# Output weights scaled in the input projection and kept in DRAM, and one add per attention unit on GpSimd

## The chip, the cores and the metric

The kernel runs on one core of a Trainium2 chip. The metric is the device time of one execution in microseconds (us); three runs were made. The trace is that of one profiled execution. Engines are named as in the profile: PE is TensorE (its weight loads are PEld), DVE is VectorE, ACT is ScalarE, POOL is GpSimd, SP is SyncE, which here issues every DMA.

## The reference, cut to what matters

One encoder layer on 2048 tokens of width 1024. All of it is float32.

```python
mod = (silu(c) @ w_ada + b_ada)                 # one row of 6*1024
shift1, scale1, gate1, shift2, scale2, gate2 = split(mod, 6)
u = adaln_modulate(x, shift1, scale1)
q, k, v, glu = split(u @ w_in, ...)             # input projection
q, k = rope(rms_norm(q)), rope(rms_norm(k))
attn = rms_norm(softmax(q @ k.T / 8) @ v)       # 8 query heads, 2 kv heads of 64
h = conv_module(glu)                            # width 31, layer norm, swish, 512x512 projection
mixed = concat([attn, h]) @ w_o                 # 1024 x 1024
x = layer_norm(ALPHA * x + gate1 * mixed)
...                                             # gated MLP with a conv of width 3, second layer norm
```

Because `gate1` is one row, `gate1 * (m @ w_o)` is `m @ (w_o * gate1)`: the kernel multiplies the columns of `w_o` with `gate1` and never multiplies `mixed`.

## The kernel before, in words

A product that needs float32 accuracy is made of three matmuls on a high and a low part of each operand. `split` (L123, L126) makes the parts: ACT copies the tile to the high part, DVE (or POOL) subtracts it for the low part.

The work runs in stages. The program is written in Python generators, and the order on every engine is set at build time by a scheduler, which places an instruction once its operands are ready in its own time model. Each engine then runs its list strictly in order, and so does SP's list of DMAs.

- **Input projection** (to about 400 us). The 16 blocks of 128 tokens go through in groups; each group makes keys, queries and the two GLU halves, and prepares the block after it. Beside it the generator `ada_later` (L277) computes the modulation rows that are needed later, `gate1` first: for each row half of 512 columns eight loads of `w_ada` into `ar` (3 buffers), eight multiply-adds on DVE into `acc`, two matmuls with ones (L293, L294), which leave the row on all 128 partitions, and a store of one partition to `mod_d` (L297). After each group it is advanced by 7 steps.
- **Attention** (about 400 to 1250 us). 16 units, numbered 0 to 15 here, each for two heads (`p`) and 512 queries (`c`). `unit_main` goes over 16 key blocks `kt`: two score products (L576, L577), an exponential on ACT into `pr` (L578, 6 buffers), and, three key blocks at a time, the products with `v` (L587). The row sums are kept in two accumulators: POOL adds 12 of the 16 `pr` into `lp` and DVE the other 4 into `ld` (L605, L608); each has one buffer. After each key block `step` advances three generators: `unit_end` of the unit before, `unit_prep` of the unit after (its score maxima: L177 on PE, L179 on DVE, then L182, L186, L188), and `conv_work`.
- `unit_end` begins with `lp + ld` on DVE (L527); two steps later PE sums it over the partitions (L535), which frees `lp` for the next unit.
- `conv_work` ends, in unit 12, with `load_wo` (L618). It loads `gate1` on all partitions, then 16 pieces of `w_o` (tile `rw`, 2 buffers). Each piece is multiplied with `gate1` on DVE (L630) and split: ACT writes `woh` (L123), DVE writes `wol` (L126).
- **Output projection, MLP, last norm** (from about 1250 us) use the split weights and are not touched.

Of the kernel before, what the change touches and what calls it, by code (L numbers as in the profile page):

```python
# [10 lines left out]
F32 = mybir.dt.float32  # L11
F32R = mybir.dt.float32r
AF = mybir.ActivationFunctionType
ALU = mybir.AluOpType
# [4 lines left out]
P = 128  # L19
D = 1024  # L20
S = 2048
NT = 16
KD = D // P
# [10 lines left out]
def layer_kernel(ctx, tc, x, cT, w_ada, b_ada, b_adaT, w_in, qg2, kg2, rope, conv_t, cmask, mmask,  # L34
# [3 lines left out]
    V, A, G, T, SY = nc.vector, nc.scalar, nc.gpsimd, nc.tensor, nc.sync  # L38
# [15 lines left out]
    mod_d = dram.tile([4, D], F32, name="mod_d")  # L54
# [2 lines left out]
    t_d = dram.tile([2, 4, P, 4, 512], F32, name="t_d")  # L57
    g_d = dram.tile([NJ, P, S], F32, name="g_d")
    w_d = dram.tile([7, P, NJ // 2, 512], F32, name="w_d")

    ident = const.tile([P, P], F32, name="ident")
    make_identity(nc, ident)
# [131 lines left out]
    with ExitStack() as ph:  # L194
# [81 lines left out]
        def ada_later():  # L276

            for i, v in enumerate((2, 3, 4, 5)):
                for h in range(2):
                    c0 = v * D + h * 512  # L280
                    acc = wka.tile([P, 512], F32, name="acc", bufs=1)
                    for k in range(KD):
                        raw = wka.tile([P, 512], F32, name="ar", bufs=3)
                        SY.dma_start(raw, w_ada[k * P:(k + 1) * P, c0:c0 + 512])
                        if k == 0:
                            V.tensor_scalar(acc, raw, cs[:, 0:1], None, op0=ALU.mult)
                        else:
                            V.scalar_tensor_tensor(acc, raw, cs[:, k:k + 1], acc, op0=ALU.mult, op1=ALU.add)
                        yield
                    br = wka.tile([P, 512], F32, name="ar", bufs=3)  # L290
                    SY.dma_start(br[0:1, :], b_ada[0:1, c0:c0 + 512])
                    ps = bank()
                    T.matmul(ps, lhsT=ones, rhs=acc, start=True, stop=False)  # L293
                    T.matmul(ps, lhsT=ones[0:1, :], rhs=br[0:1], start=False, stop=True)  # L294
                    A.activation(acc[0:1], ps[0:1], AF.Identity, bias=1.0 if v == 4 else 0.0,
                                 scale=1 / ALPHA if v == 5 else 1.0)
                    SY.dma_start(mod_d[i:i + 1, h * 512:(h + 1) * 512], acc[0:1, :])  # L297
                    yield
# [153 lines left out]
        for gi, grp in enumerate(groups):  # L452
            ks = {}
            nxt = grp[-1] + 1
            last = gi == len(groups) - 1
            for s in grp:
                ks[s] = keys(s, us[s], proj(us[s], "kv", pss[s, "kv"], hi) if gi == 0 else None)
            for s in grp:
                queries(s, us[s], ks[s][0], proj(us[s], "q", pss[s, "q"], hi) if gi == 0 else None)
                if len(grp) == 1 and nxt < NT:  # L460
                    us[nxt] = prep(nxt)
            if last:
                for s in grp:
                    keys_end(s, ks[s][1])
                for _ in bg:
                    pass
                wix.close()
                u0 = pool(rx, "u0", "right")
                gen0 = unit_prep(u0, *units[0], prep0, u0)
                next(gen0)  # L470
                gen1 = unit_prep(None, *units[1], prep1, u0)
                next(gen1)
            for i, s in enumerate(grp):
                for _ in glu(s, us[s]):
                    if last:
                        drain(gen0, 4)
                if i == 0 and len(grp) > 1 and nxt < NT:
                    us[nxt] = prep(nxt)
                if not last:
                    keys_end(s, ks[s][1])  # L480
                if gi > 0:
                    for _ in range(7):
                        next(bg, None)
            if gi == len(groups) - 2:
                us[14] = prep(14)
                us[15] = prep(15)
# [37 lines left out]
    def unit_end(p, c, po, lp, ld):  # L524
        o = wk.tile([P, 512], F32, name="o", bufs=2)
        A.activation(o, po, AF.Copy)
        V.tensor_tensor(lp, lp, ld, op=ALU.add)  # L527
        osq = wk.tile([P, 512], F32, name="osq", bufs=1)
        A.activation(osq, o, AF.Square)
        ls = wk.tile([P, 8], F32, name="ls", bufs=2)  # L530
        yield
        yield
        pl = bank()
        for i in range(2):
            T.matmul(pl[i * 64:(i + 1) * 64, :], lhsT=ones[:, 0:64], rhs=lp[:, i, :], start=True, stop=True)  # L535
        l2 = wk.tile([P, 512], F32, name="l2", bufs=1)
        A.activation(l2, pl, AF.Square, scale=EPS ** 0.5)
        V.tensor_tensor(osq, osq, l2, op=ALU.add)
        yield
        yield  # L540
        st = bank()
        for i in range(4):
            T.matmul(st[:, i * 2:i * 2 + 2], lhsT=osq[:, i * P:(i + 1) * P], rhs=blk, start=True, stop=True)
        A.activation(ls, st[:, 0:8], AF.Copy)
        G.tensor_tensor(ls, ls, mhalf[:, 0:8], op=ALU.pow)
        for _ in range(5):
            yield
        rescale(wk, o, agc[:, p:p + 1], ls)
        SY.dma_start(mix_d[p, :, c * 512:(c + 1) * 512], o)
        yield  # L550
# [67 lines left out]
    def load_wo():  # L618
        wr = pool(wrx, "wr", "right")
        wp = pool(wox, "wpC", "right")  # L620
        g1 = wp.tile([P, D], F32, name="row_g1")
        SY.dma_start(g1, mod_d[0:1].broadcast_to([P, D]))
        for k in range(KD):
            woh.append(wp.tile([P, D], F32R, name="woh%d" % k))
            wol.append(wp.tile([P, D], F32R, name="wol%d" % k))
            for h in range(2):
                sl = slice(h * 512, (h + 1) * 512)
                raw = wp.tile([P, 512], F32, name="rw", bufs=2)
                SY.dma_start(raw, w_o[k * P:(k + 1) * P, sl])
                V.tensor_tensor(raw, raw, g1[:, sl], op=ALU.mult)  # L630
                yield
                split(woh[k][:, sl], wol[k][:, sl], raw)
                yield

        def load_mix(t):
            raw = wp.tile([P, KD, P], F32, name="mr", bufs=1)
            SY.dma_start(raw, mix_d[:, :, t * P:(t + 1) * P].rearrange("k p t -> p k t"))
            mh = wp.tile([P, KD, P], F32R, name="mh", bufs=2)
            ml = wp.tile([P, KD, P], F32R, name="ml", bufs=2)
            split(mh, ml, raw, None, G)  # L640
            mixes[t] = mh, ml

        mixes["load"] = load_mix
        mixes["raw"] = [wr.tile([P, KD, P], F32, name="wr%d" % i) for i in range(2)]
        load_mix(0)
        yield
        load_mix(1)
# [771 lines left out]
```

## Time and profile before

| what | value |
|---|---|
| time of the three runs | 2818.41, 2823.8, 2823.6 us; median 2823.6 |
| profiled execution: its own time | 2820.62 us |
| profiled execution: span of the trace | 2818.8 us |
| PE busy | 2680.5 us, 95% of the span |
| DVE busy | 2213.6 us, 79% |
| POOL busy | 1246.4 us, 44% |
| mean granted clock of PE | 0.977 of full speed |

PE is the busiest engine over the whole span. A busy share over the span says little about one stage; the stages that the change touches are read one by one further down. A granted clock of 1.00 is 2.4 GHz, one of 0.50 is 1.2 GHz.

### The profile page before, as it was taken

How to read it: one execution, taken by the hardware profiler on the slowest of the kernel's cores; microseconds unless marked ns; L12 is line 12 of the kernel's file. 1: busy time of each engine (PE TensorE's matmuls, PEld its weight loads, DVE VectorE, ACT ScalarE, POOL GpSimd, SP SyncE). 2: the span in 40 equal slices, each digit the busy share in tenths (PEclk: the TensorE clock that was granted, in tenths of full speed). 3: DMA queues.
4: the chain of work that ended last, by engine and by line, in shares of the span. 5: the costliest groups of instructions: out<-in, count | busy, mean ns of one | idle time of the engine just before them, and what ended most of it. 6: DMA issues, size and time to landing. Idle time of an engine off the chain costs nothing. (4 is left out here: it accounts for less than half of the span.)

```text
span 2818.8 us, 35305 instructions
## 1 busy us (share of the span) xinstructions
PE 2680.5 (95%) x12108; PEld 2020.6 (72%) x12108; DVE 2213.6 (79%) x3188; ACT 1304.3 (46%) x2562; POOL 1246.4 (44%) x914
## 2 busy tenths in 40 slices
PE   7999999999999999899988999999999998999996
PEld 6877866766565665458867788876888887777774
DVE  7554466576858767847779999899999878989999
ACT  4433324445545455434464554555554555443542
POOL 3534436886857667534544322233231002336235
PEclk8999999999999999899999999999999999999998
DMA  8343241010101112116777433354344226545542
GB/s 274 95 138 115 76 98 33 22 34 19 31 19 27 27 38 75 42 30 187 229 214 226 150 131 116 124 175 160 130 155 139 89 91 220 158 128 147 170 148 68
DMA packets 336867, 320.59 MB, mean 114 GB/s; under 512 B 70688, under 2 KB 244128, under 8 KB 336688
## 3 DMA queue, kind: packets, MB, share of 16 engines
q1 hardware_dynamic: 336688, 318.34, 37.3%
q8 instruction: 95, 1.56, 0.2%
q14 instruction: 84, 0.69, 0.1%
HBM read 225.71 MB, written 92.55 MB: 113 GB/s over the span
## 5 line engine op out<-in xcount | busy, mean ns | idle before, releaser
L1082 PE MATMUL b<-o,wh 128*128 128x512 f32 x3696 | 1155.3, 397 | 47.2 <-ACT wh L123 18.5
L1082 PEld LDWEIGHTS b<-o,wh 128*128 128x128 f32 x3696 | 698.8, 190 | 218.3 <-ACT wh L123 23.8
L1082 PE MATMUL b<-o,wl 128*128 128x512 f32 x1848 | 719.1, 396 | 6.5 <-DVE wl L126 6.5
L123 ACT ACTIVATE wh<-wr 128x512 fp32r<-128x512 f32 (+2 forms) x456 | 252.0, 571 | 379.2 <-PE b L1082 202.4
L608 POOL TENSOR_TENSOR lp<-lp,pr 128x1024 f32<-128x1024 f32 x152 | 382.4, 2516 | 77.5 <-ACT pr L578 69.5
L1082 PEld LDWEIGHTS b<-o,wl 128*128 128x128 f32 x1848 | 350.5, 190 | 90.9 <-DVE wl L126 12.7
L578 ACT ACTIVATE pr<-b 128x512 f32<-128x512 f32 x512 | 279.1, 599 | 290.6 <-PE b L577 283.3
L179 DVE TENSOR_REDUCE mm<-b 128x1 f32<-128x512 f32 x512 | 321.4, 681 | 116.2 <-PE b L177 114.6
L126 DVE TENSOR_TENSOR wl<-wr,wh 128x512 fp32r<-128x512 f32 (+2 forms) x456 | 334.7, 746 | 10.7 <-ACT wh L123 9.9
L587 PE MATMUL b<-pr,vt 128*64 128x512 f32 x1024 | 245.1, 609 | 4.2 <-ACT pr L578 4.2
L1178 POOL TENSOR_TENSOR cb<-cb,g 128x512 f32<-128x512 f32 x44 | 75.2, 1732 | 383.6 <-DMA cb<-in_w_down_dram 383.6
L576 PE MATMUL b<-q,K 128*128 128x512 f32 x512 | 219.1, 430 | 9.5 <-DVE mm L179 5.3
L577 PE MATMUL b<-q,K 72*128 72x512 f32 x512 | 207.2, 406 | 3.0 <-DVE q L188 3.0
L177 PE MATMUL b<-K,q 128*128 128x512 f32 x512 | 166.0, 421 | 6.0 <-DVE mm L179 5.0
L587 PEld LDWEIGHTS b<-pr,vt 128*64 128x64 f32 x1024 | 66.5, 138 | 131.2 <-issue 114.1
L126 POOL TENSOR_TENSOR o<-stg,o 128x512 fp32r<-128x512 f32 x53 | 82.5, 1558 | 148.2 <-ACT o L123 146.2
L177 PEld LDWEIGHTS b<-K,q 128*128 128x128 f32 x512 | 92.4, 192 | 71.4 <-issue 34.1
L123 ACT ACTIVATE o<-stg 128x512 fp32r<-128x512 f32 x177 | 107.6, 630 | 74.8 <-DMA stg<-w_d 52.8
L1059 POOL TENSOR_TENSOR wr<-wr,wr 128x384 f32<-128x384 f32 (+1 forms) x32 | 34.8, 1089 | 241.4 <-DVE s L1056 229.9
L576 PEld LDWEIGHTS b<-q,K 128*128 128x128 f32 x512 | 99.8, 195 | 57.5 <-issue 18.7
L577 PEld LDWEIGHTS b<-q,K 72*128 72x128 f32 x512 | 100.4, 196 | 21.0 <-issue 3.4
L126 DVE TENSOR_TENSOR o<-stg,o 128x512 fp32r<-128x512 f32 x124 | 109.3, 900 | 2.7 <-ACT o L123 2.5
(259 smaller groups left out, 4891.4 us busy)
## 6 DMA issues: line engine op xcount, KB each, us to landing
wr<-in_w_up_dram SPq DMA_DIRECT2D x88, 512.0 KB
stg<-w_d SPq DMA_DIRECT2D x133, 256.0 KB
g_d<-y SPq DMA_DIRECT2D x44, 512.0 KB
w_d<-cb SPq DMA_DIRECT2D x77, 256.0 KB
wr<-g_d SPq DMA_DIRECT2D x96, 192.0 KB
ar<-in_w_ada_dram SPq DMA_DIRECT2D x64, 256.0 KB
cb<-in_w_down_dram SPq DMA_DIRECT2D x44, 256.0 KB
x<-in_x_dram SPq DMA_DIRECT2D x32, 256.0 KB
```

Source lines behind the costliest of these rows:

```text
L123: A.activation(hi, src, AF.Copy)
L126: (el or V).tensor_tensor(lo, src, hi.bitcast(F32), op=ALU.subtract)
L177: T.matmul(px, lhsT=q1[:, i * P:(i + 1) * P], rhs=K1[:, g, kc * 512:(kc + 1) * 512], start=True, stop=True)
L179: V.tensor_reduce(mm[:, h * 4 + i, kc:kc + 1], px, axis=AX, op=ALU.max)
L576: T.matmul(ps, lhsT=k1, rhs=m1, start=True, stop=False)
L577: state["s"] = T.matmul(ps, lhsT=k2, rhs=m2[0:72], start=False, stop=True).ins
L578: ex = state["exp"] = A.activation(pr[:, i, :], ps, AF.Exp, scale=0.125).ins
L587: state["pv"] = T.matmul(po[i * 64:(i + 1) * 64, :], lhsT=vt[:, kt, g * 64:(g + 1) * 64], rhs=pr[:, i, :], start=kt == 0, stop=kt == NT - ...
L608: eng.tensor_tensor(acc, acc, pr, op=ALU.add)
L1059: (V if n < NU else G).tensor_tensor(a21, a11, a21, op=ALU.subtract)
L1082: T.matmul(ps, lhsT=a[x][:, k, :], rhs=b[y][k], start=first and k == 0 and (x, y) == (0, 0), stop=k == nk - 1 and x == 1, skip_group_check ...
L1178: G.tensor_tensor(b[i, k], b[i, k], g2[:, k * 512:(k + 1) * 512], op=ALU.mult)
```

## The change

In `ada_later` the two halves of the `gate1` row are no longer stored to `mod_d`. They are copied from PSUM on all 128 partitions, and then eight pieces of `w_o` per half are loaded into `ar`, multiplied on DVE and stored to a new DRAM tensor `wo_d`, one piece per step. `load_wo` loads the finished pieces into `rw`, with 4 buffers instead of 2, and only splits them; the broadcast load of `gate1` there is gone. `ada_later` is advanced by 9 steps per group instead of 7 (it had 72 steps and has 86). In `unit_end` the add `lp + ld` moves from DVE to POOL.

```diff
+    wo_d = dram.tile([2, KD, P, 512], F32, name="wo_d")
...
                     T.matmul(ps, lhsT=ones, rhs=acc, start=True, stop=False)
                     T.matmul(ps, lhsT=ones[0:1, :], rhs=br[0:1], start=False, stop=True)
+                    if v == 2:
+                        A.activation(acc, ps, AF.Copy)
+                        for k in range(KD):
+                            raw = wka.tile([P, 512], F32, name="ar", bufs=3)
+                            SY.dma_start(raw, w_o[k * P:(k + 1) * P, h * 512:(h + 1) * 512])
+                            V.tensor_tensor(raw, raw, acc, op=ALU.mult)
+                            SY.dma_start(wo_d[h, k], raw)
+                            yield
+                        continue
                     A.activation(acc[0:1], ps[0:1], AF.Identity, bias=1.0 if v == 4 else 0.0,
                                  scale=1 / ALPHA if v == 5 else 1.0)
...
                 if gi > 0:
-                    for _ in range(7):
+                    for _ in range(9):
                         next(bg, None)
...
         A.activation(o, po, AF.Copy)
-        V.tensor_tensor(lp, lp, ld, op=ALU.add)
+        G.tensor_tensor(lp, lp, ld, op=ALU.add)
         osq = wk.tile([P, 512], F32, name="osq", bufs=1)
...
         wp = pool(wox, "wpC", "right")
-        g1 = wp.tile([P, D], F32, name="row_g1")
-        SY.dma_start(g1, mod_d[0:1].broadcast_to([P, D]))
         for k in range(KD):
...
                 sl = slice(h * 512, (h + 1) * 512)
-                raw = wp.tile([P, 512], F32, name="rw", bufs=2)
-                SY.dma_start(raw, w_o[k * P:(k + 1) * P, sl])
-                V.tensor_tensor(raw, raw, g1[:, sl], op=ALU.mult)
+                raw = wp.tile([P, 512], F32, name="rw", bufs=4)
+                SY.dma_start(raw, wo_d[h, k])
                 yield
                 split(woh[k][:, sl], wol[k][:, sl], raw)
```

Three places show how the lists of the engines change. A row is the source line, the operation, output and inputs, the tile, and how often it repeats; numbers behind a tile's name count buffers. Line numbers from `ada_later` on are 10 higher after the change, and 7 higher from `load_wo` on.

The first place is DVE's list where unit 12 ends and unit 13 begins. Before:

```order
L608 TENSOR_TENSOR ld<-ld,pr 128x1024
L527 TENSOR_TENSOR lp<-lp,ld 128x1024
L630 TENSOR_TENSOR rw<-rw,row_g_9677 128x512
L169 TENSOR_TENSOR q_9743<-b,q_9742 64x512
L630 TENSOR_TENSOR rw<-rw,row_g_9677 128x512
L169 TENSOR_TENSOR q_9752<-b,q_9751 64x512
L179 TENSOR_REDUCE mm<-b 128x1 x2
L126 TENSOR_TENSOR wol_9680<-rw,woh_9679 128x512
L179 TENSOR_REDUCE mm<-b 128x1 x4
L126 TENSOR_TENSOR wol_9680<-rw,woh_9679 128x512
L630 TENSOR_TENSOR rw<-rw,row_g_9677 128x512
L179 TENSOR_REDUCE mm<-b 128x1 x6
```

And the same place after the change:

```order
L618 TENSOR_TENSOR ld<-ld,pr 128x1024
L127 TENSOR_TENSOR wol_9741<-rw,woh_9740 128x512 x2
L170 TENSOR_TENSOR q_9802<-b,q_9801 64x512
L180 TENSOR_REDUCE mm<-b 128x1
L127 TENSOR_TENSOR wol_9832<-rw,woh_9831 128x512
L180 TENSOR_REDUCE mm<-b 128x1
L170 TENSOR_TENSOR q_9811<-b,q_9810 64x512
L127 TENSOR_TENSOR wol_9832<-rw,woh_9831 128x512
L180 TENSOR_REDUCE mm<-b 128x1 x4
L127 TENSOR_TENSOR wol_9913<-rw,woh_9912 128x512 x2
L127 TENSOR_TENSOR wol_10018<-rw,woh_10017 128x512
L180 TENSOR_REDUCE mm<-b 128x1 x2
```

The add and the multiplies are gone, and the subtractions follow each other more closely: before, the 16 of them were spread over unit 13 and the beginning of unit 14; now the last stands ahead of the last 12 of the 32 reductions `mm` of unit 13. On ACT the last of the 16 copies `woh` now has 18 of the unit's 32 exponentials behind it.

The second place is POOL's list at the end of unit 0 (`tz` are the conv's weights, `hT` its input with zeroed edges). Before:

```order
L608 TENSOR_TENSOR lp<-lp,pr 128x1024 x7
L668 MEMSET hT 128x4
L669 MEMSET hT 128x4
L676 TENSOR_TENSOR tz<-ct,cm 128x384 x4
L668 MEMSET hT 128x4
```

And after:

```order
L618 TENSOR_TENSOR lp<-lp,pr 128x1024 x7
L537 TENSOR_TENSOR lp<-lp,ld 128x1024
L675 MEMSET hT 128x4
L676 MEMSET hT 128x4
L683 TENSOR_TENSOR tz<-ct,cm 128x384 x4
```

The add of the two sums now stands in POOL's list directly behind the last sum of the unit, ahead of the conv's work.

The third place is DVE's list in one group of the input projection. Before:

```order
L384 TENSOR_TENSOR K_93<-b,K_93 64x2x128
L347 TENSOR_REDUCE kss<-ka 128x2
L348 TENSOR_SCALAR kss<-kss 128x2
L352 TENSOR_TENSOR kn<-b,krst 128x128
L375 TENSOR_TENSOR kd<-kb,kr 128x256
L347 TENSOR_REDUCE qss<-qa 128x8
L348 TENSOR_SCALAR qss<-qss 128x8
L126 TENSOR_TENSOR ul<-u,uh 128x512
```

And after:

```order
L394 TENSOR_TENSOR K_94<-b,K_94 64x2x128
L301 TENSOR_TENSOR ar<-ar,acc 128x512 x3
L357 TENSOR_REDUCE kss<-ka 128x2
L358 TENSOR_SCALAR kss<-kss 128x2
L362 TENSOR_TENSOR kn<-b,krst 128x128
L301 TENSOR_TENSOR ar<-ar,acc 128x512
L385 TENSOR_TENSOR kd<-kb,kr 128x256
L301 TENSOR_TENSOR ar<-ar,acc 128x512 x2
L357 TENSOR_REDUCE qss<-qa 128x8
L358 TENSOR_SCALAR qss<-qss 128x8
L301 TENSOR_TENSOR ar<-ar,acc 128x512
L127 TENSOR_TENSOR ul<-u,uh 128x512
```

The multiplies of `w_o` stand between the keys' work (`kss`, `kn`, `kd`) and the low parts `ul` of the next block's input; what follows a multiply on DVE waits with it.

## Rows read from the trace of the kernel before

**Rows 1.** The page's busy times: engine, us, share of the span, instructions.

```profile
PE 2680.5 (95%) x12108; PEld 2020.6 (72%) x12108; DVE 2213.6 (79%) x3188; ACT 1304.3 (46%) x2562; POOL 1246.4 (44%) x914
```

**Rows 2.** Stretches: length, PE, PEld, DVE, ACT, POOL busy us (instructions), clock, DMA.

```profile
100.00:350.00 250.00, 248.89 (x1249) 201.96 (x1248) 119.89 (x236) 89.55 (x198) 105.10 (x137) 1.00 0.33 104
741.20:786.50 45.30, 42.99 (x187) 24.80 (x186) 35.26 (x47) 23.43 (x43) 34.66 (x16) 0.96 0.09 24
1099.40:1165.90 66.50, 51.77 (x188) 28.18 (x189) 63.69 (x71) 30.61 (x56) 35.85 (x14) 0.86 0.25 78
1165.90:1211.50 45.60, 45.37 (x187) 24.26 (x184) 35.75 (x50) 22.71 (x43) 30.65 (x12) 0.94 0.05 18
```

**Rows 3.** Waits from 1090 to 1260 us: waiter, whom for, us, times, longest.

```profile
PE b L576 <- DVE mm L179: 3.4, 2, 2.8
PE b L587 <- ACT pr L578: 3.4, 2, 2.4
```

**Rows 4.** Tile `rw`: min/median/max ns of the subtractions; idle time before its instructions.

```profile
L126 DVE TENSOR_TENSOR wol<-rw,woh x16: 672/692/2280, 1104.3 to 1177.6; 128x512 fp32r<-128x512 f32 x16
...
  DVE rw L630: 18.0, 9
```

**Rows 5.** DVE's costliest groups in unit 13: busy us, mean ns, idle before.

```profile
L630 DVE TENSOR_TENSOR rw<-rw,row_g 128x512 f32<-128x512 f32 x14 | 20.3, 1448 | 0.6 <-DMA rw<-in_w_o_dram 0.6
L179 DVE TENSOR_REDUCE mm<-b 128x1 f32<-128x512 f32 x32 | 19.9, 674 | 0.0
L126 DVE TENSOR_TENSOR wol<-rw,woh 128x512 fp32r<-128x512 f32 x13 | 14.9, 1147 | 2.2 <-ACT woh L123 2.1
```

**Rows 6.** Stretches at the lower clock, columns as in group 2.

```profile
1164.30:1171.10 6.80, 5.77 (x14) 1.57 (x14) 6.62 (x11) 5.20 (x11) 0.00 (x0) 0.50 0.18 56
450.90:457.70 6.80, 4.24 (x16) 3.98 (x17) 3.70 (x5) 0.39 (x1) 0.44 (x1) 0.50 0.00 0
```

**Rows 7.** Timeline of DVE, end of unit 0: start, us, [idle before].

```profile
451.37 1.22 DVE L527 TENSOR_TENSOR lp<-lp,ld 128x1024 f32<-128x1024 f32 x1 [7.15 <-POOL lp L608]
452.63 1.28 DVE L169 TENSOR_TENSOR q<-b,q 64x512 fp32r<-64x512 f32 x2
```

**Rows 8.** Timeline of PE at the same place.

```profile
453.46 0.77 PE L695 MATMUL b<-tz,hT 128*128 128x128 f32 x2 [4.75 <-DVE q L169]
```

**Rows 9.** Line L527: min/median/max ns; what it waited for (us, times).

```profile
L527 DVE TENSOR_TENSOR lp<-lp,ld x16: 1205/1226/2114, 451.4 to 1243.4; 128x1024 f32<-128x1024 f32 x16
...
  POOL lp L608: 16.5, 6
```

**Rows 10.** Waits of PE from 440 to 900 us: us, times, longest.

```profile
PE b L186 <- DVE mz L182: 4.7, 2, 2.6
...
PE b L177 <- DVE mm L179: 2.2, 1, 2.2
PE b L576 <- DVE mm L179: 1.9, 2, 1.7
```

**Rows 11.** Tile `lp`: POOL's adds, min/median/max ns.

```profile
L608 POOL TENSOR_TENSOR lp<-lp,pr x152: 2338/2385/3281, 411.4 to 1238.4; 128x1024 f32<-128x1024 f32 x152
```

**Rows 12.** Timeline of DVE, end of unit 14.

```profile
1211.44 1.23 DVE L527 TENSOR_TENSOR lp<-lp,ld 128x1024 f32<-128x1024 f32 x1 [2.26 <-POOL lp L608]
```

**Rows 13.** Timeline of PE at the same place.

```profile
1213.28 1.08 PE L535 MATMUL b<-lp,ones 128*64 128x512 f32 x4
```

**Rows 14.** Waits of DVE from 100 to 350 us: us, times, longest.

```profile
DVE acc L286 <- DMA mod_d<-acc: 15.1, 6, 3.3
DVE acc L288 <- DMA ar<-in_w_ada_dram: 10.8, 19, 1.1
```

**Rows 15.** Timeline of POOL in unit 13.

```profile
1103.41 2.59 POOL L126 TENSOR_TENSOR ml<-mr,mh 128x1024 fp32r<-128x1024 f32 x1 [4.04 <-ACT mh L123]
```

**Rows 16.** Timeline of DVE at the same place.

```profile
1104.27 2.28 DVE L126 TENSOR_TENSOR wol<-rw,woh 128x512 fp32r<-128x512 f32 x1
```

## The prediction

> **What bounds the kernel now.** I began with the page's busy times: PE works 95% of the span [rows 1], so the time can only fall where PE waits, or runs at its lower clock. The windows by stage show where that is. From 100 to 350 us, in the input projection, PE is busy 248.89 of 250 us at full clock, and DVE only 119.89 [rows 2]: work given to DVE there has room. In attention most units are bound by PE too. Unit 6 takes 45.3 us with 187 matmuls and 42.99 us of PE; unit 13, with 188 matmuls, takes 66.5 us at a granted clock of 0.86, and there DVE is busy 63.69 us [rows 2]. So unit 13 is bound by DVE, and it is the unit in which `load_wo` runs. The list of waits says the same: PE waits there for DVE's reductions `mm`, and for exponentials [rows 3]. The exponentials are late because ACT, in order, stands at copies `woh` whose tile DVE has not multiplied yet: 18.0 us in 9 waits [rows 4]. Two thirds of the gain or loss must therefore be looked for in unit 13, the rest at the ends of the units.
>
> **Term 1, unit 13.** The multiplies L630 go: 14 of the 16 stand in this unit, 20.3 us at a mean of 1448 ns [rows 5]. One add L527 of 1.2 us goes with them. If nothing else changed, DVE would need 63.7 - 20.3 - 1.2 = 42.2 us, about the 43.0 us of PE in unit 6, and the two would be nearly balanced. But the order shows all 16 subtractions moved ahead of the last 12 reductions, so DVE is overloaded in the first part and idle in the second. What DVE has to do up to the last subtraction: 16 subtractions at 1147 ns, 18.4 us (at the median of 692 ns [rows 4], 11.1); 20 reductions at 19.9 / 32 = 0.62 us, 12.4 us [rows 5]; of the unit's other work, 63.7 - 20.3 - 19.9 - 14.9 = 8.6 us, I put two thirds there, 5.7. Together 36.5 us, or 29.2 with the short subtractions. PE's work in the same part lies between 14 of 32 exponentials' worth, 0.44 x 43.0 = 18.8 us, and 20 of 32 reductions' worth, 26.9 us; the middle is 22.9. DVE thus holds the unit up by 36.5 - 22.9 = 13.6 us at worst durations and 6.3 at best; I take 10, because POOL is busy about half of the unit (35.85 of 66.5 us [rows 2]) and the subtractions are long only beside it. Unit 13 then takes 53 us: **a gain of 13.5**. Bounds: 43.0 + 29.2 - 26.9 = 45.3 us, a gain of 21; 43.0 + 36.5 - 18.8 = 60.7, a gain of 6.
>
> **Term 2, unit 14.** Two multiplies and three subtractions still stand at its start; they leave it. PE has 187 matmuls as in unit 6 but is busy 45.37 us instead of 42.99 [rows 2], and the 6.8 us from 1164.3 run at half clock with 5.77 us of PE [rows 6], which costs half of that, 2.9. **Gain 2**, between 0 and 3.
>
> **Term 3, the end of unit 0.** DVE stands 7.15 us at L527 because POOL is behind with its sums, and the low parts `q` of the next unit are queued behind it [rows 7]; PE waits 4.75 us for them [rows 8] and then runs 6.8 us at half clock with 4.24 us of work [rows 6], another 2.1. With the add on POOL nothing on DVE waits there. `q` still needs its transposes, which PE has done a few us earlier. **Gain 5**, between 0 and 6.9. What is late next is POOL itself, by one add; but POOL then waits for PE anyway, since the sums' buffer is free only after L535.
>
> **Term 4, the other unit ends.** DVE is rid of 16 adds at 1.226 us, 19.6 us, and of 16.5 us of waiting for POOL in front of them [rows 9], of which 7.15 are in term 3. PE's waits for DVE from 440 to 900 us, without that of term 3, are 4.7 + 2.2 + 1.9 = 8.8 us [rows 10]: the most that can come back. Against it POOL gets 16 adds at 2.385 us [rows 11]. Where PE is already waiting for the sum, the add is longer by 2.385 - 1.226 = 1.16 us. The tightest place is unit 14: the add ends at 1211.44 + 1.23 = 1212.67 [rows 12], L535 starts at 1213.28 [rows 13], so 0.6 us of slack against 1.16: PE loses about 0.6 there. In the other units the slack is about as large as the add is longer, or larger. If every one of the 16 passed its 1.16 us on, 18.6 us would be lost. I take **a gain of 1.5**, with -12 and +8 as ends: nearer to the upper end, since only one place has no slack.
>
> **Term 5, the input projection.** Added: 16 multiplies on DVE (a two-input pass over 128x512 like the subtraction, 0.69 us at the median [rows 4], 11 us), 16 loads and 16 stores of 256 KB on SP. Removed: two of the eight `mod_d` stores, on whose kind DVE waits up to 3.3 us each [rows 14]. DVE has 130 us free in those 250 us, and its existing waits for DMAs, 15.1 + 10.8 us [rows 14], do not reach PE. So **zero**, covered by the distance of a block between preparing a block and using it; without that cover up to 26 (below).
>
> **Sum.** 13.5 + 2 + 5 + 1.5 = 22 us. The profiled execution took 2820.62 us of its own, so 2798.6; it is 3.0 below the median shown (2823.6), and the runs spread over 5.4. I put the median of the changed kernel at **2800 us**, about 0.8% below. The measurement can tell about 0.2%, 5.6 us, from no change.
>
> **A rule against the rows.** A subtraction that started 0.9 us into a POOL operation took 2.28 us: POOL's ran from 1103.41 to 1106.00 [rows 15], DVE's from 1104.27 to 1106.55 [rows 16], 0.55 us past its end, nearly its undisturbed 0.69. The Trainium skill (SBUF — State Buffer, "Who interferes with whom") says that a VectorE instruction with two SBUF inputs and a GpSimd instruction that reads SBUF exclude each other for the whole instruction, whichever came first; by that rule, the trace agrees here. By the rule a subtraction that falls at random on POOL's 54% busy time would take about 0.69 + 0.54 x 1.2 = 1.34 us instead of the 1.147 of the row, the 16 would cost 3 us more, and the sum would be 19 us instead of 22.
>
> **Rivals.**
> *Half of it stays (15%).* In unit 13 the wait changes its name: ACT, rid of 18.0 us of waiting for the multiply, waits instead for loads whose buffer is only free after DVE's subtraction four pieces before. For it speaks the density of the new order; against it that DVE waited only 0.6 us for these loads so far [rows 5]. Term 1 falls to about 4: 2809 us.
> *POOL's adds hold DVE up (9%).* Each 2.4 us add on POOL can hold a two-input operation of DVE, as in groups 15 and 16; if two of three pass 1.16 us to PE, term 4 is -12: 2813 us. The rule of the Trainium skill named above would make this possible in every unit.
> *Nothing measurable (12%).* DVE stays the bound in unit 13 at 60.7 us, term 3 is eaten by POOL's delay, and the stages after 1250 us, whose order the scheduler has also shuffled, lose some us: 2820.
> *Slower (8%).* One mechanism: in the input projection each `ar` buffer now goes through load, multiply and store before it is loaded again. A multiply can wait for a store (3.3 at most) and a load (1.1) [rows 14], 4.4 us x 16 = 70 us, and `kd` and `ul`, which PE needs, stand behind it on DVE. As three buffers overlap, I expect a third of it, 23 us, hidden like the 26 there now. It decides from the point where more than 28 of the 70 us reach PE (22 gained, 5.6 to be seen); with 50 of them the time is 2828 us.
>
> **Chances and range.** The forecast (2789 to 2807) has 56%. Range: 2789 takes terms 1 and 3 near their upper bounds (8 and 2 more, 2790); 2816 includes the first two rivals. The chance of faster is the forecast's, both partial rivals' and none of the others: 80%; same 12%; slower 8%.
>
> **What would show it.** Right: unit 13, from the end of unit 12's sum to the next, near 53 us; no wait of `woh` for a multiply; no wait of PE near 453 us, and a clock of 1.00 there; PE still busy over 248 us from 100 to 350. Wrong: `woh` waiting for DMAs, PE waiting at L535 in several units, or PE idle in the input projection.

## The result and the profile after

The changed kernel takes 2806.29 us (median of 6 runs, 2801.87 to 2811.55), against 2823.69 for the kernel before in the same session: a ratio of 0.9942, 95% interval [0.9929, 0.9954], 17.4 us less. The profiled execution took 2801.87 us of its own at a span of 2800.1, 18.75 below that of before (2820.62); it was the lowest of its six. Line numbers after L301 are higher by 10 in the changed kernel, those behind `load_wo` by 7.

The page's busy times (columns as in [rows 1]): PE is busy for 96% of the span; DVE is busy 6 us less than before, POOL 32 us more.

```profile
PE 2676.4 (96%) x12108; PEld 2016.9 (72%) x12108; DVE 2207.4 (79%) x3172; ACT 1299.2 (46%) x2562; POOL 1278.4 (46%) x930
```

The stretches that answer to those of [rows 2]: the input projection, unit 6, unit 13 and unit 14.

```profile
100.00:350.00 250.00, 248.90 (x1243) 200.79 (x1242) 132.62 (x251) 89.06 (x200) 103.84 (x136) 1.00 0.45 138
734.50:779.60 45.10, 42.20 (x190) 24.00 (x189) 38.07 (x45) 23.47 (x45) 37.32 (x19) 1.00 0.10 25
1093.90:1146.80 52.90, 47.62 (x184) 25.70 (x183) 48.39 (x57) 30.70 (x57) 37.34 (x15) 0.90 0.30 91
1146.80:1189.00 42.20, 42.20 (x186) 23.36 (x184) 32.34 (x42) 20.36 (x39) 31.45 (x14) 1.00 0.02 7
```

Unit 13 again, cut at the start of its last subtraction (1127.4 us):

```profile
1093.90:1127.40 33.50, 28.70 (x100) 14.55 (x98) 33.22 (x40) 21.61 (x40) 21.04 (x9) 0.85 0.45 136
1127.40:1146.80 19.40, 18.91 (x86) 11.14 (x85) 15.17 (x19) 9.09 (x17) 16.30 (x7) 1.00 0.04 15
```

Unit 13 is 52.9 us long where it was 66.5. DVE's busy time there fell by 15.3 us and is still above PE's 47.62: DVE's work is still the larger, by less. Up to the last subtraction DVE is busy for 33.22 of 33.50 us; behind it PE is busy for 18.91 of 19.40 us at clock 1.00. Unit 14 runs at clock 1.00 and PE is never idle in it. In the input projection DVE does 12.7 us more and PE is as busy as before, to 0.01 us.

In unit 13 the groups of DVE are the reductions and the 15 subtractions that now stand in it, no shorter than they were in [rows 5]:

```profile
L180 DVE TENSOR_REDUCE mm<-b 128x1 f32<-128x512 f32 x32 | 20.0, 675 | 0.3 <-PE b L178 0.3
L127 DVE TENSOR_TENSOR wol<-rw,woh 128x512 fp32r<-128x512 f32 x15 | 17.4, 1187 | 0.0
```

Tile `rw` (answers to [rows 4]): the 18.0 us in which ACT stood at a multiply are gone, and 5.0 us of waiting for loads are new.

```profile
L127 DVE TENSOR_TENSOR wol<-rw,woh x16: 671/678/2875, 1091.6 to 1127.4; 128x512 fp32r<-128x512 f32 x16
...
  DMA rw<-wo_d: 5.0, 3
```

PE's longest waits from 1085 to 1240 us follow, against 3.4 and 3.4 us in [rows 3]; all rows of that list come to 7.6 us, where those from 1090 to 1260 us came to 17.2 before:

```profile
PE b L178 <- DVE mm L180: 1.6, 1, 1.6
PE b L586 <- DVE q L170: 1.5, 1, 1.5
PE b L586 <- DVE mm L180: 1.4, 1, 1.4
```

At the end of unit 0, DVE's timeline shows `q` with 2.81 us of waiting for ACT ahead of it instead of 7.15 for POOL [rows 7], and POOL's shows the add after six sums without a pause. PE, which waited 4.75 us there [rows 8], is busy 14.59 of the 15 us from 445 to 460, at clock 1.00:

```profile
447.84 1.28 DVE L170 TENSOR_TENSOR q<-b,q 64x512 fp32r<-64x512 f32 x2 [2.81 <-ACT q L169]
```

```profile
435.80 16.39 POOL L618 TENSOR_TENSOR lp<-lp,pr 128x1024 f32<-128x1024 f32 x6
452.27 2.38 POOL L537 TENSOR_TENSOR lp<-lp,ld 128x1024 f32<-128x1024 f32 x1
```

```profile
445.00:460.00 15.00, 14.59 (x88) 10.58 (x87) 7.17 (x15) 9.08 (x17) 12.84 (x10) 1.00 0.17 38
```

The add itself (line L537, answers to [rows 9]), with what it waited for and who waited for it:

```profile
L537 POOL TENSOR_TENSOR lp<-lp,ld x16: 2357/2379/2718, 452.3 to 1222.0; 128x1024 f32<-128x1024 f32 x16
...
  DVE ld L618: 12.7, 8
...
  PEld b L545: 0.4, 1
```

And among PE's waits from 440 to 900 us (answers to [rows 10]) there is one that was not there, for `cl_e`:

```profile
PE b L187 <- DVE mz L183: 3.6, 3, 2.6
...
PE b L178 <- DVE mm L180: 2.2, 1, 2.2
PE b L586 <- DVE cl_e L90: 2.0, 1, 2.0
```

To set kernels side by side I take a unit's length as the time from its first exponential `pr` (L578 before, L588 after) to that of the next unit, from the timeline of ACT, and "attention" as the time from the first exponential of unit 0 to the start of the last of all. Units that are not shown differ by 0.8 us at most from before, but for unit 0 (up to 1.6 shorter) and unit 6 in the kernel with the add alone (1.1 longer). The first line is before, the second the change, the rest the experiments below.

```
                          start  unit 1  unit 8  unit 11  unit 13  unit 14  attention  after it
before                    404.3   69.8    50.8    51.7     66.1     43.3     835.4     1579.1
changed                   405.0   63.1    54.3    49.7     52.8     40.7     813.3     1581.8
changed, run again        407.9   63.1    54.4    49.7     52.4     40.7     813.0     1581.9
weights only              406.7   69.5    50.8    51.7     55.0     40.7     821.5     1583.9
add only                  408.9   63.1    52.8    49.7     68.6     42.1     830.1     1584.2
two buffers               408.3   63.1    54.4    49.7     57.3     40.7     819.0     1578.3
add of units[7] on DVE    408.4   63.1    50.8    49.7     52.7     40.7     807.7     1583.2
split kept                412.3   63.1    54.3    49.7     43.5     41.3     803.9     1580.0
added work twice          440.6   63.1    54.2    49.7     52.9     40.7     812.9     1580.1
split kept, units[7]      415.0   63.1    50.8    49.7     43.5     41.3     801.3     1576.5
twice, five buffers       406.2   63.1    54.4    49.7     53.0     40.7     814.7     1585.0
multiply twice            405.7   63.1    54.4    49.7     52.4     40.7     813.5     1586.2
split kept, spread        409.0   63.1    50.8    49.7     43.4     41.3     801.8     1581.0
```

Three things are read from it before any theory. Unit lengths repeat to a few tenths from execution to execution. The start of attention and the time after it do not: kernels with the same input projection begin at 404.3 and 408.9 (before, add only), or at 405.0, 407.9 and 406.7 (changed, again, weights only), and the time after attention, whose code is the same in all of them, lies anywhere within 10 us; four of them also have the same order on PE there and take 1579.1, 1584.2, 1580.0 and 1576.5 us (before, add only, split kept, and that with `units[7]`). The 2.7 us that the change seems to lose after attention is therefore not something that one profile can show. And the scatter of the start arises early. From PE's fourth pair of transposes of `kd` (L381 before, L391 after), near 125 us, to the first exponential it takes 280.3 us before, 279.9 with the add alone, and 280.1, 280.2 and 280.5 (changed, again, weights only). That stretch is used below to tell what work in the input projection costs.

### The profile page after: what moved, and what is told of

Read it like the earlier page. It is cut to its first block, busy times and chain, and to the rows that moved or that the text cites. A ratio compares the mean times of both kernels' runs of the same rounds, so it can differ in the third digit from the quotient of the medians.

```text
span 2800.1 us, 35379 instructions
## 1 busy us (share of the span) xinstructions
PE 2676.4 (96%) x12108; PEld 2016.9 (72%) x12108; DVE 2207.4 (79%) x3172; ACT 1299.2 (46%) x2562; POOL 1278.4 (46%) x930
## 5 line engine op out<-in xcount | busy, mean ns | idle before, releaser
L588 ACT ACTIVATE pr<-b 128x512 f32<-128x512 f32 x512 | 278.7, 598 | 284.1 <-PE b L587 271.7
L127 DVE TENSOR_TENSOR wl<-wr,wh 128x512 fp32r<-128x512 f32 (+2 forms) x456 | 339.6, 756 | 12.5 <-ACT wh L124 11.4
L597 PEld LDWEIGHTS b<-pr,vt 128*64 128x64 f32 x1024 | 66.5, 138 | 128.9 <-issue 111.8
```

Of the source, the lines that this page charges most:

```text
L127: (el or V).tensor_tensor(lo, src, hi.bitcast(F32), op=ALU.subtract)
L588: ex = state["exp"] = A.activation(pr[:, i, :], ps, AF.Exp, scale=0.125).ins
L597: state["pv"] = T.matmul(po[i * 64:(i + 1) * 64, :], lhsT=vt[:, kt, g * 64:(g + 1) * 64], rhs=pr[:, i, :], start=kt == 0, stop=kt == NT - ...
```

## The experiments

**The change once more**, on the chip on which three others were timed.

> The changed kernel itself, once more, timed beside the three that follow, so that they can be compared with it on one chip: 16 to 20 us below the kernel before; its units, from the first exponential of one to that of the next, within 0.5 us of the first profile (unit 1 63.1, unit 8 54.3, unit 13 52.8), while the start of attention and the time after it may differ by some us.

2804.35 us, ratio 0.9929 [0.9916, 0.9942]. The units of the table came out as before to 0.4 us.

**Weights only.** The add is back on VectorE:

```
-        G.tensor_tensor(lp, lp, ld, op=ALU.add)
+        V.tensor_tensor(lp, lp, ld, op=ALU.add)
```

> The changed kernel with the add of the row sums back on VectorE (L537), so that only the weights are moved. Theory (gain = multiplies out of units 13 and 14, 15.9 us, plus the add at the end of unit 0, 6.7 us, less 3.5 us that POOL's add costs at the start of unit 8): unit 13 stays near 53 us, unit 14 near 41, unit 1 goes back to about 70 us with PE waiting 4 to 5 us near 453 us, unit 8 goes back to about 51. Whole: 14 to 16 us below the kernel before, 2 to 4 above the changed one. Rival A (unit 13 was bound by the adds and POOL, not by the multiplies): unit 13 above 60 us and less than 8 us gained. Rival B (work in the input projection costs something that other gains hide): the start of attention is more than 2 us later than before and less than 11 us are gained.

2814.07 us, ratio 0.9958 [0.9942, 0.9975], 11.8 us below before where I had said 14 to 16. Attention is 13.9 us shorter, a little under what the theory gave; units 1, 8 and 14 did as it said. PE waits 4.4 us for `q` near 453 us. Unit 13 is 55.0, not 53: of its 13.3 us the moved weights bring 11.1, and 2.2 come only when the add leaves DVE too. With those and 2.0 us in unit 11, which the theory had left out, attention is 8.2 us longer than in the changed kernel, not 2 to 4. Rival A is out: over 8 us are gained, and unit 13 is below 60. Of rival B one sign came: attention begins 2.4 us later, but within the scatter, and from 125 us on the input projection takes 280.5 us where it took 280.3; the gain, 11.8, is just above its limit of 11.

**Add only.** The kernel before, with that one line changed the other way.

> The kernel before with only the add of the row sums moved to GpSimd. Theory: unit 1 from 69.8 to about 63 us (no wait of PE near 453 us), unit 8 some 3 us longer, unit 13 unchanged within 2 us of 66.1; whole 2 to 5 us below the kernel before, and with the weights alone it adds up to the 17 to 19 us of the change. Rival A (the two parts are not independent: the add also helps unit 13, where DVE is the bound): unit 13 down by 3 us or more. Rival C (POOL's adds cost more at the other ends than they save at unit 0): slower than before by 2 us or more.

2823.24 us, ratio 0.9992 [0.9982, 1.0003]: no difference that can be measured, although attention is 5.2 us shorter in the profile. Unit 1 gives 6.7, unit 11 gives 2.0, unit 8 loses 2.0 and unit 13 loses 2.5. Unit 11 gains as unit 1 does: before, `q` stood behind the add on DVE there, and PE waited for it:

```profile
1002.25 0.50 PE L576 MATMUL b<-q,K 128*128 128x512 f32 x1 [0.96 <-DVE q L169]
```

With the add on POOL that wait is gone, with the weights alone it is not. Rival A is not borne out as stated: with the old multiplies in place the add on POOL makes unit 13 longer, and only with the new weights shorter. The parts are not independent there. In the trace ACT's waits for a multiply came to 23.2 us instead of 18.0, and PE's longest wait for an exponential to 5.9 instead of 3.1; why was not pursued. In attention the two parts give 13.9 + 5.2 = 19.1 us alone and 22.1 together; that the times add up to 17 to 19 us, as I had expected, two medians of 11.8 and 2.6 don't show.

**Two buffers.**

```
-                raw = wp.tile([P, 512], F32, name="rw", bufs=4)
+                raw = wp.tile([P, 512], F32, name="rw", bufs=2)
```

> The changed kernel with two buffers for the loads rw instead of four, as the kernel before had. Theory (it is the multiplies that were taken away): unit 13 within 1 to 2 us of 52.8, although ACT waits longer for the loads; whole within 3 us of the changed kernel. Rival (the gain comes from the denser loads, which need four buffers): ACT's waits of woh for DMAs go from 5 us to 15 or more, and unit 13 goes to 58 us or above, whole 5 us or more above the changed kernel.

The theory's 1 to 2 us were too few. Unit 13 is 57.3 us, 4.5 more, and ACT's wait for loads is what the rival said, three times that of the changed kernel (tile `rw` of this kernel):

```profile
L637 SPq DMA_DIRECT2D rw<-wo_d x16: 319/320/480, 1092.2 to 1146.0; - x16
...
  DMA rw<-wo_d: 15.1, 11
```

So about a third of unit 13's gain hangs on the four buffers; the rest comes without them, from the multiplies and the add. The whole, 2806.08 us and a ratio of 0.9935 [0.9917, 0.9952], doesn't show the 4.5 us: the interval is 10 us wide, and this kernel was not timed beside the changed one. The counterpart, four buffers in the kernel before, wasn't tried; the row of gates that the change removes is as large as the two buffers that it adds.

**One add back.** Unit 8 had become 3.5 us longer. The changed kernel's DVE there, then POOL, then PE, and the stretch that follows:

```profile
839.39 1.99 DVE L734 TENSOR_SCALAR hc<-hc,cl_mv,cl_r 128x512 f32<-128x512 f32 x1
841.30 0.17 DVE L101 BATCH_NORM_AGGREGATE cl_mv<-cl_st 128x2 f32<-128x6 f32 x1
841.39 2.49 DVE L734 TENSOR_SCALAR hc<-hc,cl_mv,cl_r 128x512 f32<-128x512 f32 x1
843.80 0.73 DVE L532 SCALAR_TENSOR_TENSOR ot<-ot,cgc,b 128x512 f32<-128x512 f32 x1
844.46 0.14 DVE L90 TENSOR_SCALAR cl_e<-cl_mv 128x1 f32<-128x1 f32 x1
```

```profile
838.71 2.38 POOL L618 TENSOR_TENSOR lp<-lp,pr 128x1024 f32<-128x1024 f32 x1
841.17 2.42 POOL L537 TENSOR_TENSOR lp<-lp,ld 128x1024 f32<-128x1024 f32 x1
```

```profile
844.59 0.50 PE L586 MATMUL b<-q,K 128*128 128x512 f32 x1 [1.98 <-DVE cl_e L90]
```

```profile
845.70:849.10 3.40, 3.30 (x10) 2.26 (x9) 3.40 (x7) 1.50 (x3) 0.00 (x0) 0.50 0.39 95
```

Both `hc` end 0.3 us after a POOL add ends; the second one began 0.22 us after the moved add did. PE waits 1.98 us and then has 3.30 us of work at half clock, 1.65 lost: 3.6 in all. The experiment moves this one add back:

```
-        G.tensor_tensor(lp, lp, ld, op=ALU.add)
+        (V if (p, c) == units[7] else G).tensor_tensor(lp, lp, ld, op=ALU.add)
```

> The changed kernel with the add of one unit, units[7], back on VectorE; the other fifteen stay on GpSimd. Theory (POOL's add at the start of unit 8 held DVE's tensor_scalar hc for 2.49 us instead of 0.50, and cl_e and ot behind it, for which PE waited and then ran at half clock): unit 8 from 54.3 back to about 51 us, hc at about 0.5 us, whole 2 to 4 us below the changed kernel. Rival (the order alone makes the wait, or PE would have waited for something else): unit 8 stays above 53 us, whole within 1 us of the changed kernel.

The same two `hc` of DVE, in the same order, then:

```profile
840.92 1.99 DVE L734 TENSOR_SCALAR hc<-hc,cl_mv,cl_r 128x512 f32<-128x512 f32 x1
842.83 0.17 DVE L101 BATCH_NORM_AGGREGATE cl_mv<-cl_st 128x2 f32<-128x6 f32 x1
842.92 0.51 DVE L734 TENSOR_SCALAR hc<-hc,cl_mv,cl_r 128x512 f32<-128x512 f32 x1
```

The first, beside the same sum of POOL as before, still takes 1.99 us; the second, now beside nothing, 0.51. Unit 8 is 50.8 us again and PE's wait for `cl_e` is gone. The time is 2802.44 us, ratio 0.9921 [0.9905, 0.9937]: below the changed kernel's 0.9942 and 0.9929, with intervals that overlap; the unit's length decides. So it is POOL's add that holds DVE here, and not the order. `hc` has one 128x512 input in SBUF, not two. The Trainium skill (SBUF — State Buffer, "Who interferes with whom") says that `tensor_scalar` too can enter a mode in which it and GpSimd exclude each other. The trace agrees that it is held, 2.49 us against 0.51; in which mode `hc` runs, no row shows.

**The split moved as well.** High and low parts are both made in the input projection and kept:

```
+                            hl = [wka.tile([P, 512], F32R, name="wo" + n, bufs=1) for n in "hl"]
+                            split(*hl, raw)
+                            for n in range(2):
+                                SY.dma_start(wo_d[n, h, k], hl[n].bitcast(F32))
...
-                split(woh[k][:, sl], wol[k][:, sl], raw)
+                SY.dma_start(woh[k][:, sl].bitcast(F32), wo_d[0, h, k])
+                SY.dma_start(wol[k][:, sl].bitcast(F32), wo_d[1, h, k])
```

> The changed kernel with the split moved too: high and low parts of the product are made in the input projection and both kept in DRAM; load_wo only loads. Out of units 12 to 14 go 16 copies on ACT (9.9 us) and 16 subtractions on DVE (17.4 us); in the input projection as many are added, with single buffers that wait for their stores, and twice the bytes are stored and loaded. Theory (unit 13 is still held up by DVE's subtractions and the waits behind them; the input projection has room): unit 13 from 52.8 to 43 to 46 us, start of attention within 3 us, whole 6 to 10 us below the changed kernel. Rival A (unit 13 is by now bound by something else, POOL's sums or the exponentials): unit 13 stays above 50 us and less than 3 us are gained. Rival B (the input projection's room is used up: PE waits for DVE there): the start of attention is 5 us or more later and the gain is lost.

2799.91 us, ratio 0.9922 [0.9908, 0.9937], 4.4 below the changed kernel run again. Unit 13:

```profile
1099.50:1143.00 43.50, 41.16 (x186) 23.96 (x184) 29.14 (x42) 22.52 (x43) 30.46 (x13) 1.00 0.61 209
```

With the subtractions gone the unit falls to PE's time and the clock stays at 1.00, at twice the bytes; rival A is out. ACT's 16 copies went with them, and no run takes away one without the other; but PE's three longest waits in unit 13 of the changed kernel were for DVE, and ACT was busy for 30.70 of 52.90 us. 8.9 us were gained in unit 13 and only 4.4 stayed: attention begins 4.4 us later, and from 125 us on the input projection takes 284.4 us instead of 280.2. Rival B is half right: from 200 to 250 us, where PE of the changed kernel is busy without a break, it now is not, and the clock falls for a moment:

```profile
200.00:250.00 50.00, 47.91 (x225) 38.04 (x224) 29.64 (x58) 16.98 (x39) 19.45 (x25) 0.97 0.60 185
```

So what is the room in the input projection?

**The added work twice.** Each of the 16 steps loads, multiplies and stores a second time, to a place that nobody reads.

> The changed kernel with the work added to the input projection done twice: each of the 16 steps loads the piece of the weights again, multiplies it again and stores it to a second place in DRAM that nobody reads (16 more multiplies on DVE, 16 more loads and 16 more stores of 256 KB). Theory (that work is hidden): start of attention within 3 us of the changed kernel's 405.0 to 408.5, PE busy still above 247 of the 250 us from 100 to 350, whole within 3 us of the changed kernel. Rival (the ring of three buffers ar, which goes through load, multiply and store, passes waits on to PE): start of attention 5 to 25 us later, with PE waiting for kd or ul.

The theory, and the reason that term 5 of the prediction gave, fails here: 2837.02 us, ratio 1.0046 [1.0033, 1.0059], slower than the kernel before. Attention begins 32.7 us after that of the changed kernel run again. PE's timeline shows both places where it waits:

```profile
183.40 2.05 PE L295 MATMUL b<-acc,ones 128*128 128x512 f32 x2 [11.65 <-DVE acc L290]
...
243.70 2.05 PE L295 MATMUL b<-acc,ones 128*128 128x512 f32 x2 [12.99 <-DVE acc L290]
```

and the stretches around them that it then runs at the lower clock, with DVE busy for half of the time only:

```profile
150.00:200.00 50.00, 38.35 (x179) 30.30 (x178) 27.41 (x51) 11.78 (x27) 14.25 (x20) 0.83 0.70 221
200.00:250.00 50.00, 37.01 (x166) 28.65 (x165) 25.80 (x44) 12.42 (x26) 15.82 (x19) 0.86 0.70 204
```

PE does not wait for `kd` or `ul`, as I had thought, but for `acc`. The product of `ones` with `acc` is a matmul of the modulation itself; it has its fixed place among PE's projections, and behind a half of `w_o` the next `acc` is collected through the same buffers `ar`. In the changed kernel PE comes to that matmul at 168.61 us:

```profile
168.61 1.02 PE L294 MATMUL b<-acc,ones 128*128 128x512 f32 x2
```

and DVE's last addition to that `acc` was

```profile
156.46 0.75 DVE L289 SCALAR_TENSOR_TENSOR acc<-ar,cs,acc 128x512 f32<-128x512 f32 x1 [0.45 <-DMA ar<-in_w_ada_dram]
```

so it was ready 168.61 - 157.21 = 11.4 us early. That slack is the room. For the two matmuls that follow the two halves of `w_o`, with PE's wait where there is no slack, and the time from the fourth transposes of `kd` to attention:

```
                          slack of the first, second; us     from 125 us     start of attention
changed                       11.4, 11.8                        280.1           405.0
changed, run again            10.5, 10.4                        280.2           407.9
multiply twice                 6.5,  3.9                        280.4           405.7
twice, five buffers            1.7,  1.6                        280.3           406.2
split kept                     1.2, none, waits 2.09            284.4           412.3
split kept, units[7]           1.8, none, waits 3.07            287.7           415.0
added work twice              none, waits 11.65 and 12.99       312.7           440.6
```

In the four kernels that have slack at both, this stretch is as long as before the change (280.3). The two waits in the kernels that keep the split:

```profile
217.60 1.10 PE L294 MATMUL b<-acc,ones 128*128 128x512 f32 x2 [2.09 <-ACT uh L124]
...
217.73 2.05 PE L294 MATMUL b<-acc,ones 128*128 128x512 f32 x2 [3.07 <-DVE acc L289]
```

Both begin 0.14 to 0.15 us after the last addition to `acc`, like those of the doubled work. The first is put down to ACT's `uh`, which ended 0.07 us after that addition; either would have held it.

**What in it uses up the slack** is told apart by two kernels: the doubled work with five buffers `ar` instead of three, and the changed kernel with only the multiply done twice.

> The kernel that does the added work of the input projection twice (2837 us, attention begins at 440.6 us, PE waits 11.65 and 13.0 us for the last acc of a half), with five buffers ar instead of three; the extra products are again read by nobody. Theory (each step's way through load, multiply and store in a ring of three is what made acc late, 2.9 us for each of the eight extra steps of a half): with five buffers more steps overlap, PE's waits for acc fall from 24.6 us to under 10, attention begins at 408 to 422 us, whole 15 to 30 us below the doubled kernel. Rival (the order of SP's queue, where each store waits for its multiply ahead of the next loads, or DVE's own time, sets the pace): PE still waits 20 us or more for acc, attention begins after 435 us.

> The changed kernel with only the multiply done twice on DVE, into a tile of its own that nobody reads (16 more multiplies at 0.69 us, no more loads or stores). Theory (the way through the ring costs, not DVE's time): the slack between the last acc of a half and PE's matmul on it falls from 11.4 and 11.8 us by 6 us at most, PE does not wait for acc, attention begins within 3 us of 405.0 to 408.5, whole within 3 us of the changed kernel. Rival (DVE's time is what ran out when everything was doubled): the slack is gone, PE waits for acc, attention begins 5 us or more later.

With five buffers the doubled work is hidden: 2805.79 us, ratio 0.9945 [0.9923, 0.9967], and PE does not wait for `acc`. The rival is out as stated: the stores still wait for their multiplies in SP's queue, and DVE does the same work. The order on DVE shifts by some rows with the buffers, so that ring and order are not wholly apart. With the multiply alone doubled, 2806.32 us, ratio 0.9947 [0.9928, 0.9966], the slack falls by 4.9 and 7.9 us (I had said 6 at most; against the changed kernel run again it is 4.0 and 6.5), and the time by nothing. In eight steps, then, the extra multiplies cost 4 to 8 us of slack, and the whole doubled step with three buffers 11.4 + 11.65 = 23.1 and 11.8 + 12.99 = 24.8, about 3 us a step; in the second half PE, at the lower clock, came 3.8 us later by itself. With five buffers it costs 9.7 and 10.2. So the larger part is the way through load, multiply and store, which more buffers overlap.

**Both improvements together**: the split kept, and the add of `units[7]` on VectorE.

> The kernel with high and low parts kept in DRAM, and the add of units[7] back on VectorE: the two improvements that the runs point to, together. Theory: they add up, unit 8 near 50.8 and unit 13 at 43 to 46 us; whole 9 to 14 us below the changed kernel, 26 to 32 below the kernel before. Rival (they do not add up, or the split in the input projection is not free): less than 6 us below the changed kernel.

2796.94 us, ratio 0.9905 [0.9892, 0.9918]: 7.4 us below the changed kernel run again and 26.6 below before. In attention they add up (units 8 and 13 at 50.8 and 43.5), 11.7 us in all; against it stand 7.5 us in the input projection (287.7 instead of 280.2), where PE waits 3.07 us for `acc` and then runs at the lower clock. That the split there is not free, as the rival has it, is so; its limit of 6 us was not reached.

**That version with the steps spread**: a second `yield` after each step, and ten draws instead of nine.

> The kernel with both parts of the split kept in DRAM and the add of units[7] on VectorE (2796.9 us, attention begins at 415.0 us), with each of the 16 added steps spread over two draws and ten draws instead of nine at a time. Theory (there the slack of 11.4 and 11.8 us before PE's matmul on acc has fallen to 1.8 and 0.1, and PE waits and slows there): the slack comes back to 5 us or more in both halves, no wait of uh or kn on top, attention begins at 407 to 411 us, whole 3 to 7 us below 2796.9. Rival (the later start comes from ACT's copies or DMA traffic, not from acc): attention still begins after 413 us and the time stays within 2 us.

2796.45 us, ratio 0.9912 [0.9895, 0.9929]: no better. The slack of the first matmul rose to 21.8 us, that of the second came to no more than 0.3, since only the first half got more time: its matmul now comes 64.4 us after the one before it instead of 43.5, the second's 43.5 instead of 46.7. PE did not wait for `acc`, and attention began at 409.0, 6 us earlier where the scatter is 4.6. From 125 us on the input projection takes 284.8 us: 2.9 less than without the spread, 4.6 more than in the changed kernel. The loss has moved: from 335 to 340 us PE now runs at clock 0.50, where it was 1.00. The time doesn't show the difference, and whether the spread helps stays open.

## Why the prediction was right, point by point

Forecast 2800 us, range 2789 to 2816; measured 2806.29. The sign, the places and most sizes held.

- *Term 1, unit 13, 13.5 us:* measured 13.3, to the 53 us that I named. The mechanism is shown by the split kept: with DVE's subtractions (and ACT's copies) gone too, the unit falls to 43.5, PE's own time. The two parts are also as I had them: up to the last subtraction, where I put 29.2 to 36.5 us of DVE's work, DVE is busy for 33.2, and behind it PE is the bound. That the middle of my 6.3 and 13.6 us came out to 0.2 is luck: DVE's work in the unit is 48.4 us and not 42.2, since 15 subtractions stand in it and the three sums `ld` are slower (3.4 and twice 2.1 us instead of 2.8 and twice 1.2). The make-up differs: weights alone 11.1, the add leaving DVE 2.2, and without the four buffers 4.5 of it are lost.
- *Term 2, unit 14, 2 us:* 2.6; with the weights alone as well.
- *Term 3, end of unit 0, 5 us:* 6.7, near the upper bound; it comes with the add alone, and not with the weights alone.
- *Term 4, the other ends, 1.5 us gained:* the term that was mis-sized. Unit 8 lost 3.5, unit 11 gained 2.0, unit 6 some 0.7, which may be scatter: about 1 us lost. I had counted slack at L535 only. The 0.6 us that I forecast for unit 14 did not come, PE's matmul begins 0.62 us after the add there as before; 0.4 us came elsewhere, at 737.2 us behind the add of unit 5. What I gave as a rival, a POOL add that holds a DVE operation, is what cost unit 8 its 3.5 us, and in an operation with one input, while I had tied it to two. The trace of before already showed such operations held by POOL's sums (last section).
- *Term 5, the input projection, nothing:* right in size (from 125 us on 280.1 and 280.2 us, against 280.3), wrong in its reason. I named DVE's 130 us of free time and a block's distance as cover. The cover is 10 to 12 us of slack at two matmuls on `acc`; doubling the work costs 32.7 us. My slower rival had the mechanism (three buffers through load, multiply and store) and nearly the price (4.4 us a step; 3 were measured), but the wrong instruction, and it needed twice the work.
- *The sum:* terms 1 to 4 came to about 22 us, as forecast, and attention is 22.1 us shorter. The execution gained 18.75, the medians 17.4 and 19.2; the 3 to 5 us between lie ahead of 125 us and behind attention, which scatter that much between executions of kernels that don't differ there. I can't attribute them.

Of the rivals, *half of it stays* did not come: 5.0 us of waiting for loads took the place of 18.0, though with two buffers it is 15.1. *Nothing measurable* is what the add alone gave. *The rule against the rows* gave 1.34 us for a subtraction and 19 us for the sum. The 15 in unit 13 took 1.187 us on average, near the 1.147 of the row; that the whole time fell by 17.4 to 19.2 us is no sign for the rule, since attention fell by 22.1.

## What to carry to other kernels

Free time of an engine is not room: find the instruction of the bounding engine that will meet the moved work's result, and read how long before it that result is ready now; here 11 us, with DVE half idle. When work goes through a ring of buffers by load, operation and store, the operation can be the smaller part of its price: here eight steps cost 23 to 25 us of slack with three buffers and about 10 with five, and the multiplies alone 4 to 8. And when an operation is moved to GpSimd, look at what VectorE reads from SBUF beside each new instance: sixteen moves gained in units 1 and 11 and lost in unit 8, and the one loser could be moved back.

## What the runs showed of the hardware that was not expected

A 128x512 `tensor_scalar` on VectorE with its input and output in SBUF took 0.51 us alone and 2.49 us when it began 0.22 us after a 2.42 us GpSimd add of two SBUF tiles; it ended 0.3 us after that add. In the same kernel two reductions `mm`, whose input `b` is in PSUM, took 1.28 us together although GpSimd's sum began at 838.71, in the middle of them; their mean in unit 13 is 675 ns each.

```profile
838.20 1.28 DVE L180 TENSOR_REDUCE mm<-b 128x1 f32<-128x512 f32 x2
```

The rows were there before the change: six of the 16 `hc` took 1.11 to 2.63 us, each of them begun after a sum of POOL had begun and ended 0.28 to 0.29 us after it; one that began 0.30 us ahead of a sum took 0.55. The sum and two `hc` of unit 8 before, one held and one not:

```profile
846.01 2.37 POOL L608 TENSOR_TENSOR lp<-lp,pr 128x1024 f32<-128x1024 f32 x1
846.69 1.98 DVE L727 TENSOR_SCALAR hc<-hc,cl_mv,cl_r 128x512 f32<-128x512 f32 x1
848.68 0.50 DVE L727 TENSOR_SCALAR hc<-hc,cl_mv,cl_r 128x512 f32<-128x512 f32 x1
```
